# Seven-product stage of a decoder layer: deviation ahead of the first column tile, first pair's weights split there, products on banks apart

## The chip, the core and the metric

One Trainium2 chip, one core of it. The metric is the device time of one execution in microseconds (us); of several executions the median counts.

## The reference, cut to what matters

One layer of a decoder works on 520 tokens (512 of a prompt, 8 of decoding) with 1024 channels in fp32. The change touches the last of its sub-layers alone:

```python
h3 = rms_norm(x, lw['norm_ffn_g'])
x = x + jnp.square(jax.nn.relu(h3 @ lw['w_up'])) @ lw['w_down']      # 1024 -> 4096 -> 1024
```

Ahead of it come a mixing layer and a cross attention, which end with `x = x + om @ w_xo`.

## The kernel before, in words

All activations lie channel by channel: a tile is 128 channels (partitions) by 520 tokens, in two halves of 260. Each fp32 factor is cut into a high and a low part of type fp32r (`hilo` for tokens: ScalarE copies the high part, VectorE subtracts; `split_weights` for weights), and a product is made of three matmuls, high by high, high by low, low by high (`mm3`, L263). A weight tile is 128 x 1024. Its low part is made in one of two ways: `low` on VectorE (L178), or, for `wup` and `wdn`, a negated copy by ScalarE (L221) to which a DMA that GpSimd issues adds the weights from memory (L222). `weights` keeps LA = 3 entries of a written order split ahead.

The stage (from L1375 on) has 32 column tiles of `w_up`, in eight groups of four, and after each group four calls of `down`, each with one tile of `w_down` for two of the eight output tiles. A `down` has 48 matmuls.

- Group 0: four column tiles by plain products (`run("wup", i, ...)`, 48 matmuls each). They use tokens that aren't divided by their deviation yet; `post_up` does that afterwards: Relu (L1423), times `Rf` (L1427), Square (L1417), `hilo`. `Rf` is made by `rstd` in `post_up(0)`: four summing matmuls (L286) over the squares in `acc`, then ScalarE (L293 to L297) and VectorE (L298, L299).
- `forms` (L1391) makes the token side of the other groups, in four steps: per step two tiles times gain and `Rf` (L1396), four sums of halves (L1404 to L1407), and the cutting of all seven operands into high and low. FTB of its tiles lie in the pool `fp`, the others among the 37 tiles of `HL`.
- Groups 1 to 7: two calls of `up_pair` each. A pair is two column tiles by two token halves, made by a scheme of seven half-size products in place of eight (`product`, 12 matmuls each, in the order a, b, e, c, d, f, h), with VectorE's sums (`add`, L1450; L1475, L1476) between them. `split_pair` prepares its weights: two raw tiles `w` loaded by the queue SP issues (L184), four sums (L191), and the cutting into high and low (L197, L178).

PSUM has eight banks: two `g` tiles of two banks, three `m` tiles of one, one `d` tile of one. In a pair b and e are the two banks of one `g` tile, f and h those of another, a, c, d are `m` tiles. In a `down` one output tile is a `g` tile and the other is two `m` tiles; `post_down` adds them to the residual (L1492 for `g`, L1488 twice for `m`).

The order of each engine's instructions is fixed when the program is built, by a list scheduler that goes by program order, by `high_priority` (which moves a block ahead by AHEAD = 60 places) and by its own model of when an operand is ready. Each engine then works its list in order. Raw weight tiles share three buffers (`WB[0]`), the high and the low parts of single tiles three each, the sums' high and low parts three (`WB2`).

Of the kernel before, what the change touches and what calls it, by code (L numbers as in the profile page):

```python
# [9 lines left out]
F32 = mybir.dt.float32  # L10
# [7 lines left out]
P = 128  # L18
# [5 lines left out]
KT = 8  # L24
# [4 lines left out]
LA = 3  # L29
HLB = 37  # L30
WB2 = 3
FTB = 9
CR = "k0 k1 q0 q1 q2 q3 k2 v0 v1 k3 v2 v3"
ZS = [0, 0, 0, 1, 0, 1, 1, 1, 1, 1, 1, 1, 1, 1, 1, 1, 0, 1, 1, 1, 0, 1, 1, 0, 1, 0]
WARM = 2
# [62 lines left out]
def layer(ctx: ExitStack, tc: tile.TileContext, I: dict, O: dict):  # L98
# [13 lines left out]
    def gtile():  # L112
        return pg.tile([P, 2, 512], F32, tag="g", name="g")

    def mtile():
        return pm.tile([P, 512], F32, tag="m", name="m")
# [4 lines left out]
    def T(dt=F32, n=NT, bufs=TB):  # L121
        return tp.tile([P, n], dt, tag="t", name="t", bufs=bufs)
# [39 lines left out]
    CP = (0, 2, 1, 3)  # L162
    order += [("wup", i) for i in range(4)] + [("wdn", c) for c in CP]
    for g in range(1, 8):
        order += [("pair", 2 * g), ("pair", 2 * g + 1)] + [("wdn", 4 * g + c) for c in CP]
    order.reverse()
    ahead = []

# [10 lines left out]

    def split_pair(i):  # L180

        w = [wp.tile([P, KT, P], F32, tag="w", name="w", bufs=WB[0]) for _ in range(2)]
        for t, j in zip(w, (2 * i, 2 * i + 1)):
            SP.dma_start(out=t, in_=I["wup"][j].rearrange("p (k c) -> p k c", k=KT))  # L184
        lo4, hi4 = slice(0, 4), slice(4, 8)
        A11, A12, A21, A22 = w[0][:, lo4], w[0][:, hi4], w[1][:, lo4], w[1][:, hi4]
        pa, pb = [fp.tile([P, KT, P], F32, tag="p", name="p", bufs=2) for _ in range(2)]
        P1, P3, P2, P4 = pa[:, lo4], pa[:, hi4], pb[:, lo4], pb[:, hi4]

        def plus(out, a, b):  # L190
            free.add(V.tensor_tensor(out=out, in0=a, in1=b, op=ALU.add).ins.name)  # L191

        def split(src, pool, tag, bufs):
            shape = [P, src.shape[1], P]
            h = pool.tile(shape, F32R, tag="wh" + tag, name="wh", bufs=bufs)
            l = pool.tile(shape, F32R, tag="wl" + tag, name="wl", bufs=bufs)
            S.copy(h, src)  # L197
            low(l, src, h)
            return [(h[:, n:n + 4], l[:, n:n + 4]) for n in range(0, src.shape[1], 4)]

        a11, a12 = split(w[0], wp, "", WB[1])
        plus(P1, A21, A22)
        plus(P2, P1, A11)
        plus(P4, P2, A12)
        p2, p4 = split(pb, fp, "2", WB2)
        plus(P3, A11, A21)
        p1, p3 = split(pa, fp, "2", WB2)
        a22, = split(A22, fp, "3", 1)
        return a11, a12, a22, p1, p2, p3, p4

    def split_weights(name, i):
        if name == "pair":
            return split_pair(i)
        src = I[name][i]
        w = wp.tile([P, KT, P], F32, tag="w", name="w", bufs=WB[0])
        SP.dma_start(out=w, in_=src.rearrange("p (k c) -> p k c", k=KT))
        wh = wp.tile([P, KT, P], F32R, tag="wh", name="wh", bufs=WB[1])
        wl = wp.tile([P, KT, P], F32R, tag="wl", name="wl", bufs=WB[2])
        S.copy(wh, w)  # L219
        if name in ("wup", "wdn"):  # L220
            S.activation(wl, w, AF.Copy, scale=-1.0)  # L221
            GP.dma_start(out=wl, in_=src.rearrange("p (k c) -> p k c", k=KT), accum_op=ALU.add)  # L222
        else:
            low(wl, w, wh)
        return wh, wl
# [85 lines left out]
    def rstd(mat, srcs, n, y, v=None):  # L311

        v, a = v if v is not None else T(), T()
        rsqrt(colsum(mat, srcs), n, v, y, a[:, 0:NT])
        return v
# [1075 lines left out]
    def forms():  # L1391

        for k in range(4):
            n, m, t, u = T(), T(), T(), T()
            for o, i in ((n, k), (m, k + 4)):
                V.scalar_tensor_tensor(out=o, in0=x2[i], scalar=col("gffn", i), in1=Rf, op0=ALU.mult, op1=ALU.mult)  # L1396
            B11, B12, B21, B22 = n[:, A0[1]], n[:, A1[1]], m[:, A0[1]], m[:, A1[1]]
            if k % 2 == 0:
                b11 = form(2)
            sl = slice(k % 2 * H2, k % 2 * H2 + H2)  # L1400
            hilo(B11, b11[0][:, sl], b11[1][:, sl])
            X["B11", k] = b11[0][:, sl], b11[1][:, sl]
            N1, T2, T3, T4 = t[:, A0[1]], t[:, A1[1]], u[:, A0[1]], u[:, A1[1]]
            V.tensor_tensor(out=N1, in0=B11, in1=B12, op=ALU.subtract)  # L1404
            V.tensor_tensor(out=T2, in0=B22, in1=N1, op=ALU.add)
            V.tensor_tensor(out=T3, in0=B22, in1=B12, op=ALU.subtract)
            V.tensor_tensor(out=T4, in0=T2, in1=B21, op=ALU.subtract)  # L1407
            for src, names in ((t, ("N1", "T2")), (u, ("T3", "T4")), (m, ("B21", "B22"))):
                hi, lo = form(2)
                hilo(src, hi, lo)  # L1410
                for j, s in zip(names, (A0[1], A1[1])):
                    X[j, k] = hi[:, s], lo[:, s]
            yield
# [6 lines left out]
    def post_up(i):  # L1420
        def post(ps):
            r = T()
            S.activation(two(r), gv(ps), AF.Relu)  # L1423
            if i == 0:
                rstd(ones, [acc], D, T(), Rf)
                flows.append(forms())
            V.tensor_tensor(out=r, in0=r, in1=Rf, op=ALU.mult)  # L1427
            ups[0][i] = HL(), HL()
            rest(r, ups[0][i])
            yield  # L1430
        return post
# [4 lines left out]
            xh, xl = X[x, k]  # L1436
            PE_last[0] = mm3([(ps, (slice(None), slice(None)))], w[0][:, k], w[1][:, k], xh, xl, k == 0, k == 3)

    def up_pair(p):

        a11, a12, a22, p1, p2, p3, p4 = weights("pair", p)
        g, n = p // 2, p % 2 * 2
        a, c, d, be, fh = mtile(), mtile(), mtile(), gtile(), gtile()
        a, b, c, d, e, f, h = (x[:, 0:H2] for x in (a, be[:, 0], c, d, be[:, 1], fh[:, 0], fh[:, 1]))
        t, u, v = T(), T(), T()
        s1, u2, u3, c21, c22 = t[:, A0[1]], t[:, A1[1]], u[:, A0[1]], v[:, A0[1]], v[:, A1[1]]

        def add(out, x, y, op=ALU.add):
            with tc.high_priority(offset=AHEAD):
                V.tensor_tensor(out=out, in0=x, in1=y, op=op)  # L1450

        product(a, a11, "B11")
        if fresh[0]:
            advance()
        with tc.high_priority(offset=AHEAD):
            S.copy(s1, a)
        product(b, p2, "T2")
        add(u2, s1, b, ALU.subtract)
        product(e, p3, "T3")
        add(u3, e, u2)  # L1460
        product(c, p1, "N1")
        add(c22, c, u3)
        add(u2, c, u2)
        product(d, a22, "T4")
        add(c21, d, u3)
        with tc.high_priority(offset=AHEAD):
            S.activation(v, v, AF.Relu, scale=-1.0)
            ups[g][n + 1] = HL(), HL()
            rest(v, ups[g][n + 1])
        product(f, a12, "B21")  # L1470
        product(h, p4, "B22")

        def post():
            r = T()
            V.tensor_tensor(out=r[:, A0[1]], in0=f, in1=s1, op=ALU.add)  # L1475
            V.tensor_tensor(out=r[:, A1[1]], in0=h, in1=u2, op=ALU.add)  # L1476
            S.activation(r, r, AF.Relu)
            ups[g][n] = HL(), HL()
            rest(r, ups[g][n])
            yield  # L1480
        take(post())

# [15 lines left out]
    def down(g, cp):  # L1498

        W = weights("wdn", 4 * g + cp)  # L1500
        cs = (2 * cp, 2 * cp + 1)
        pss = [gtile(), [mtile(), mtile()]]

        def part(n, ks, first, last):
            for i, k in enumerate(ks):
                gemm(pss[n], (W[0][:, 4 * n:], W[1][:, 4 * n:]), ups[g][k:k + 1], first=first and i == 0,
                     last=last and i == len(ks) - 1, k0=k)

        if cp == CP[0] and g:
            for n in range(2):  # L1510
                part(n, (0, 1, 3), True, False)
            for n in range(2):
                part(n, (2,), False, True)
                take(post_down(g, cs[n])(pss[n]))
        elif g == 7 and cp == CP[-1]:
            part(0, range(4), True, True)
            take(post_down(g, cs[0])(pss[0]))
            gemm(pss[1], (W[0][:, 4:], W[1][:, 4:]), ups[g], apart=True)
            take(post_down(g, cs[1])(pss[1]))
        else:  # L1520
            for n in range(2):
                part(n, range(4), True, True)
                take(post_down(g, cs[n])(pss[n]))

    for i in range(4):
        run("wup", i, x2s, post_up(i))
    go()
    for g in range(8):
        for p in (2 * g, 2 * g + 1) if g else ():
            up_pair(p)  # L1530
        if g:
            flush()
        for c in CP:
            down(g, c)
# [99 lines left out]
```

## Time and profile before

| | us |
|---|---|
| median of 3 runs | 1054.37 |
| the three runs | 1052.58, 1054.37, 1057.49 |
| the profiled execution | 1050.55 |
| its span, first to last instruction | 1048.9 |

The profiled execution is the one that all rows below come from. PE is TensorE's matmuls, PEld its weight loads, DVE VectorE, ACT ScalarE, POOL GpSimd, SP the engine that issues plain loads. A row of the timeline begins with start and duration in us, and ends with the idle time of its engine ahead of it, and what ended that. A matmul's row lasts longer than the distance to the next one, since matmuls overlap.

### The profile page before, as it was taken

The page shows a single profiled execution, that of the slowest core. Times are in us where ns is not written, and L with a number is a line of the kernel's source. Part 1 is how long each engine was busy: PE and PEld are TensorE (multiplying, and loading weights), DVE is VectorE, ACT ScalarE, POOL GpSimd, SP SyncE. Part 2 cuts the span into 40 slices and gives each one's busy share as a digit, 9 for nine tenths or more (in the row PEclk, how much of TensorE's full clock was granted, in tenths as well). Part 3 has the DMA queues.
Part 4 walks back from the last instruction along what each step waited for, and adds up shares of the span by engine and source line. Part 5 has one row for each costly group of instructions (what it writes and reads, how often), then busy time and mean ns, then how long its engine had stood idle before and what let it go on. Part 6 is the DMA issues. An engine that isn't in the chain of part 4 may idle for free.

```text
span 1048.9 us, 21539 instructions
## 1 busy us (share of the span) xinstructions
PE 1027.3 (98%) x8266; PEld 944.3 (90%) x8266; DVE 660.8 (63%) x1220; ACT 537.1 (51%) x876; POOL 173.2 (17%) x303
## 2 busy tenths in 40 slices
PE   9999999999999999999999999998999999999998
PEld 8977877789988889889999986997999999999998
DVE  7757677677555666434776687679465565656553
ACT  7755567854221235314455686684646446464452
POOL 1333443231223323320000000010000000000000
PEclk9999999999999999999999999999999999999999
DMA  8877986575557767762622575385556565665644
GB/s 295 313 247 246 260 284 218 170 201 168 181 192 243 246 204 222 236 197 81 212 85 98 193 247 184 86 168 130 143 148 139 155 140 121 153 147 147 157 102 122
DMA packets 62665, 190.97 MB, mean 182 GB/s; under 512 B 10209, under 2 KB 13026, under 8 KB 62434
## 3 DMA queue, kind: packets, MB, share of 16 engines
q0 software_dynamic: 25984, 87.07, 32.0%
q1 hardware_dynamic: 36578, 102.52, 28.9%
q8 instruction: 65, 1.06, 0.4%
q14 instruction: 38, 0.31, 0.1%
HBM read 183.94 MB, written 5.61 MB: 181 GB/s over the span
## 4 chain that ended last, share of the span: by engine, by line
PE 71%; DVE 10%; DMA 9%; ACT 6%; issue 2%; SPq 0%; DVEq 0%; ACTq 0%
PE g L263 50%; PE m L263 10%; DMA w<-in_wup 7%; PE d L600 3%; DVE p L191 3%; PE d L548 2%; PE m L286 1%; DMA w<-in_win 1%; ACT wh L219 1%; DVE wl L178 1%; PE g L1171 1%; DVE hl L146 1%; ACT wl L221 1%; DMA wl<-in_wdn 1%; DVE hl L1492 1%
## 5 line engine op out<-in xcount | busy, mean ns | idle before, releaser
L263 PE MATMUL g<-hl,wh 128*128 128x260 f32 x3664 | 609.9, 285 | 5.0 <-DVE hl L146 1.8
L263 PEld LDWEIGHTS g<-hl,wh 128*128 128x128 f32 x3664 | 511.4, 189 | 23.3 <-issue 7.0
L263 PE MATMUL g<-hl,wl 128*128 128x260 f32 x1832 | 385.2, 283 | 1.4 <-DMA wl<-in_wdn 1.4
L263 PEld LDWEIGHTS g<-hl,wl 128*128 128x128 f32 x1832 | 289.1, 189 | 1.8 <-DMA wl<-in_wdn 1.6
L219 ACT CAST wh<-w 128x1024 fp32r<-128x1024 f32 x126 | 131.8, 1047 | 244.0 <-PE g L263 116.3
L178 DVE TENSOR_TENSOR wl<-w,wh 128x1024 fp32r<-128x1024 f32 (+1 forms) x118 | 136.4, 1157 | 33.3 <-ACT wh L219 31.0
L263 PE MATMUL m<-hl,wh 128*128 128x260 f32 x736 | 127.8, 283 | 3.6 <-DVE hl L1488 3.6
L263 PEld LDWEIGHTS m<-hl,wh 128*128 128x128 f32 x736 | 105.7, 188 | 4.8 <-DVE hl L1488 4.8
L513 POOL DMA_DIRECT2D pg<-in_vc x128 | 68.8, 538 | 176.3 <-issue 78.6
L513 POOL DMA_DIRECT2D pg<-in_kc x128 | 68.9, 539 | 144.8 <-issue 99.3
L263 PE MATMUL m<-hl,wl 128*128 128x260 f32 x368 | 84.5, 283 | 1.2 <-DMA wl<-in_wdn 1.2
L222 POOL DMA_DIRECT2D wl<-in_wdn x32 | 27.6, 864 | 311.5 <-ACT wl L221 188.6
L475 DVE TENSOR_TENSOR t<-g,R 128x520 f32<-128x520 f32 x48 | 33.4, 695 | 64.1 <-PE g L263 64.1
L197 ACT CAST wh<-p 128x1024 fp32r<-128x1024 f32 x28 | 28.8, 1048 | 84.2 <-DVE p L191 58.2
L146 DVE TENSOR_TENSOR hl<-t,hl 128x520 fp32r<-128x520 f32 (+3 forms) x65 | 42.6, 657 | 33.5 <-ACT hl L145 33.2
L263 PEld LDWEIGHTS m<-hl,wl 128*128 128x128 f32 x368 | 61.0, 188 | 1.4 <-DMA wl<-in_wdn 1.4
L145 ACT CAST hl<-t 128x520 fp32r<-128x520 f32 (+3 forms) x65 | 37.8, 588 | 13.5 <-DVE t L486 11.3
L882 DVE SCALAR_TENSOR_TENSOR hl<-uc,cols,hl 128x512 f32<-128x512 f32 x60 | 41.2, 745 | 0.0
L221 ACT ACTIVATE wl<-w 128x1024 fp32r<-128x1024 f32 x36 | 37.9, 1053 | 0.0
L178 DVE TENSOR_TENSOR wl<-p,wh 128x1024 fp32r<-128x1024 f32 x28 | 33.7, 1223 | 5.6 <-ACT wh L197 5.6
L191 DVE TENSOR_TENSOR p<-w 128x512 f32<-128x512 f32 x28 | 19.3, 690 | 25.6 <-DMA w<-in_wup 25.6
L222 POOL DMA_DIRECT2D wl<-in_wup x4 | 3.5, 866 | 188.1 <-DVE ss L1199 176.2
(297 smaller groups left out, 1221.7 us busy)
## 6 DMA issues: line engine op xcount, KB each, us to landing
pg<-in_kc POOLq DMA_DIRECT2D x128, 256.0 KB, 4.4
pg<-in_vc POOLq DMA_DIRECT2D x128, 256.0 KB, 4.0
w<-in_win SPq DMA_DIRECT2D x56, 512.0 KB, 4.6
w<-in_wup SPq DMA_DIRECT2D x32, 512.0 KB, 3.9
w<-in_wdn SPq DMA_DIRECT2D x32, 512.0 KB, 3.9
wl<-in_wdn POOLq DMA_DIRECT2D x32, 512.0 KB, 7.9
w<-in_wo SPq DMA_DIRECT2D x8, 512.0 KB, 3.3
hl<-in_cmk SPq DMA_DIRECT2D x16, 256.0 KB, 5.8
```

Of the source, the lines that this page charges most:

```text
L145: S.copy(hi, src)
L146: V.tensor_tensor(out=lo, in0=src, in1=f(hi), op=ALU.subtract)
L178: free.add(V.tensor_tensor(out=wl, in0=w, in1=f(wh), op=ALU.subtract).ins.name)
L191: free.add(V.tensor_tensor(out=out, in0=a, in1=b, op=ALU.add).ins.name)
L219: S.copy(wh, w)
L221: S.activation(wl, w, AF.Copy, scale=-1.0)
L222: GP.dma_start(out=wl, in_=src.rearrange("p (k c) -> p k c", k=KT), accum_op=ALU.add)
L263: m = PE.matmul(o, lhsT=w, rhs=x[sl], start=first and n == 0, stop=last and n == 2)
L475: V.tensor_tensor(out=two(t), in0=gv(ps), in1=two(Rt), op=ALU.mult)
L513: last.append(GP.dma_start(out=dst, in_=src[bass.ds(pid, 1)].rearrange("o p f -> p o f")))
L600: PE.matmul(ps[32 * i:32 * i + 32, :], lhsT=Dt[:, n, :], rhs=vp[:, i, :], start=n == 0, stop=n == 15)
L882: V.scalar_tensor_tensor(out=y[:, 0:NP], in0=u[:, k:k + NP], scalar=cw[:, k:k + 1], in1=y[:, 0:NP], op0=ALU.mult, op1=ALU.add)
```

## The change

- `rstd` moves out of `post_up(0)` to ahead of the first column tile, under `high_priority`.
- `split_pair(2)`, the weights of the first pair, is called there too. Its raw tiles lie in the pool `fp`, in two buffers of their own (so do those of every even pair; odd pairs stay with the three shared ones), and the parts of its first raw tile lie with those of the sums. FTB falls from 9 to 5 to make room.
- Column tiles 0 and 1 run interleaved (`pair`): for each of the eight input tiles first the matmuls of one, then of the other. `forms` is stepped at written places: after them, after tile 2, and twice after tile 3.
- `wup` in group 0 gets its low part on VectorE, not by ScalarE and a DMA.
- In a pair, a goes to the `d` tile, b, c, e to `m` tiles, d to a `g` tile of its own; f and h share one as before.
- For the second pair of a group Relu and Square of one of the results become one VectorE instruction. In group 0 the first `down` takes the last column tile last, for both output tiles.

```diff
-FTB = 9
+FTB = 5
-        order += [("pair", 2 * g), ("pair", 2 * g + 1)] + [("wdn", 4 * g + c) for c in CP]
+        order += [("pair", p) for p in (2 * g, 2 * g + 1) if p > 2] + [("wdn", 4 * g + c) for c in CP]
     def split_pair(i):
-        w = [wp.tile([P, KT, P], F32, tag="w", name="w", bufs=WB[0]) for _ in range(2)]
+        w = [(wp if i % 2 else fp).tile([P, KT, P], F32, tag="w", name="w", bufs=WB[0] if i % 2 else 2) for _ in range(2)]
-        a11, a12 = split(w[0], wp, "", WB[1])
+        a11, a12 = split(w[0], wp, "", WB[1]) if i > 2 else split(w[0], fp, "2", WB2)
     def split_weights(name, i):
-        if name in ("wup", "wdn"):
+        if name == "wdn":
     def post_up(i):
-            if i == 0:
-                rstd(ones, [acc], D, T(), Rf)
-                flows.append(forms())
-    def up_pair(p):
-        a11, a12, a22, p1, p2, p3, p4 = weights("pair", p)
+    def up_pair(p, W):
+        a11, a12, a22, p1, p2, p3, p4 = W
-        a, c, d, be, fh = mtile(), mtile(), mtile(), gtile(), gtile()
-        a, b, c, d, e, f, h = (x[:, 0:H2] for x in (a, be[:, 0], c, d, be[:, 1], fh[:, 0], fh[:, 1]))
+        a, b, c, e, d, fh = dtile(), mtile(), mtile(), mtile(), gtile(), gtile()
+        a, b, c, d, e, f, h = (x[:, 0:H2] for x in (a, b, c, d[:, 0], e, fh[:, 0], fh[:, 1]))
...
-            S.activation(r, r, AF.Relu)
             ups[g][n] = HL(), HL()
-            rest(r, ups[g][n])
+            if n:
+                V.scalar_tensor_tensor(out=r, in0=r, scalar=0.0, in1=r, op0=ALU.max, op1=ALU.mult)
+                hilo(r, *ups[g][n])
+            else:
+                S.activation(r, r, AF.Relu)
+                rest(r, ups[g][n])
     def down(g, cp):
-        if cp == CP[0] and g:
+        if cp == CP[0]:
+            late = 2 if g else 3
             for n in range(2):
-                part(n, (0, 1, 3), True, False)
+                part(n, [k for k in range(4) if k != late], True, False)
             for n in range(2):
-                part(n, (2,), False, True)
+                part(n, (late,), False, True)
-    for i in range(4):
-        run("wup", i, x2s, post_up(i))
+    with tc.high_priority(offset=AHEAD):
+        rstd(ones, [acc], D, T(), Rf)
+    first_pair = split_pair(2)
+    made = forms()
+    pair([("wup", 0), ("wup", 1)], x2s, [post_up(0), post_up(1)])
+    next(made)
+    run("wup", 2, x2s, post_up(2))
+    next(made)
+    run("wup", 3, x2s, post_up(3))
     go()
+    next(made)
+    next(made)
+    next(made, None)
     for g in range(8):
         for p in (2 * g, 2 * g + 1) if g else ():
-            up_pair(p)
+            up_pair(p, first_pair if p == 2 else weights("pair", p))
```

## Rows read from the trace of the kernel before

**Rows 1.** The page: span, busy time by engine, and the raw weight loads of `w_up`.
```profile
span 1048.9 us, 21539 instructions
PE 1027.3 (98%) x8266; PEld 944.3 (90%) x8266; DVE 660.8 (63%) x1220; ACT 537.1 (51%) x876; POOL 173.2 (17%) x303
...
w<-in_wup SPq DMA_DIRECT2D x32, 512.0 KB, 3.9
```

**Rows 2.** Three windows: length, busy time and count by engine, clock, DMA share, GB/s.
```profile
664.05:681.30 17.25, 17.25 (x143) 17.25 (x144) 12.34 (x18) 12.93 (x19) 1.76 (x2) 1.00 0.50 127
...
708.59:729.55 20.96, 15.84 (x123) 14.94 (x123) 20.68 (x38) 12.32 (x18) 1.69 (x2) 1.00 0.58 127
776.55:999.03 222.48, 219.52 (x1800) 216.97 (x1800) 132.62 (x231) 113.40 (x151) 17.28 (x20) 1.00 0.59 143
```

**Rows 3.** Chain of waits, a piece near its end: start, duration, engine, line, count.
```profile
1037.05 2.87 PE m L263 x24
```

**Rows 4.** Waits of PE from 700 us on: total, times, longest.
```profile
PE m L263 <- DVE hl L1488: 3.6, 6, 0.8
PE g L263 <- DVE hl L146: 1.8, 1, 1.8
PE g L263 <- DMA wl<-in_wdn: 1.4, 1, 1.4
PE m L263 <- DMA wl<-in_wdn: 1.2, 1, 1.2
PE g L263 <- ACT hl L145: 0.7, 1, 0.7
```

**Rows 5.** Timeline, third product of pair 2, and the start of pair 4.
```profile
738.10 0.42 DVE L1450 TENSOR_TENSOR t<-t,g 128x260 f32<-128x260 f32 x1
...
738.58 0.51 PE L263 MATMUL g<-x,wh 128*128 128x260 f32 x2
...
779.42 0.40 PE L263 MATMUL m<-x,wh 128*128 128x260 f32 x2
...
780.16 0.76 DVE L1488 TENSOR_TENSOR x<-m,x 128x260 f32<-128x260 f32 x2
```

**Rows 6.** Timeline at the end of group 1, DVE and PE.
```profile
773.06 0.69 DVE L191 TENSOR_TENSOR p<-w 128x512 f32<-128x512 f32 x1 [3.35 <-DMA w<-in_wup]
...
776.08 0.76 DVE L1488 TENSOR_TENSOR hl<-m,hl 128x260 f32<-128x260 f32 x2
...
776.55 0.63 PE L263 MATMUL m<-hl,wh 128*128 128x260 f32 x3 [0.62 <-DVE hl L1488]
```

**Rows 7.** Timeline of group 0, several engines.
```profile
692.40 0.70 DVE L298 TENSOR_TENSOR t<-t,R 128x520 f32<-128x520 f32 x1 [6.94 <-ACT t L297]
...
708.45 0.59 ACT L1423 ACTIVATE t<-g 128x520 f32<-128x520 f32 x1
...
718.37 0.52 PE L263 MATMUL g<-hl,wh 128*128 128x260 f32 x2 [1.77 <-DVE hl L146]
...
722.30 0.86 POOL L222 DMA_DIRECT2D wl<-in_wdn  x1 [12.88 <-ACT wl L221]
...
729.55 0.51 PE L263 MATMUL g<-hl,wl 128*128 128x260 f32 x2 [1.41 <-DMA wl<-in_wdn]
```

**Rows 8.** Groups by shape, 681.3 to 735 us: count, busy us, mean ns, idle before.
```profile
L146 DVE TENSOR_TENSOR hl<-t,hl 128x520 fp32r<-128x520 f32 x13 | 9.2, 705 | 0.0
...
L219 ACT CAST wh<-w 128x1024 fp32r<-128x1024 f32 x7 | 7.3, 1046 | 8.7 <-PE m L263 6.4 <-PE g L263 1.4 <-ACT t L1198 0.7
...
L1396 DVE SCALAR_TENSOR_TENSOR t<-hl,cols,R 128x520 f32<-128x520 f32 x4 | 3.0, 761 | 0.0
...
L191 DVE TENSOR_TENSOR p<-w 128x512 f32<-128x512 f32 x4 | 2.8, 695 | 0.9 <-DMA w<-in_wup 0.9
...
L178 DVE TENSOR_TENSOR wl<-w,wh 128x1024 fp32r<-128x1024 f32 x2 | 2.4, 1216 | 0.0
...
L1404 DVE TENSOR_TENSOR t<-t 128x260 f32<-128x260 f32 x4 | 1.7, 429 | 0.0
```

## The prediction, on record before the changed kernel ran

> **What bounds the kernel.** Read the page first: TensorE's matmuls are busy for 1027.3 of 1048.9 us [rows 1], so time can only come from the matmuls' count, their pace, or gaps between them. The change keeps every matmul. The windows then give the granted clock, 1.00 in each [rows 2], the 2.4 GHz level, so nothing is to be had there. Pace: 143 matmuls in 17.25 us without a gap are 0.1206 us each [rows 2], 24 in 2.87 are 0.1196 [rows 3]; I take 0.120. With it the windows show where matmuls are not back to back. Five groups, 1800 matmuls (per group 2 x 84 + 4 x 48 = 360 by the code), want 216.0 us and took 222.5: **1.3 us lost per group**. From 708.59 to 729.55, in group 0, 123 matmuls want 14.8 us and took 21.0: **6.2 us lost** [rows 2].
>
> The list of waits says on what [rows 4]. Six times PE waits for L1488, the reading of two `m` tiles: 3.6 us idle, 0.6 each. Idle time understates a wait: two matmuls last 0.40, so a row of one is 0.28 long and runs 0.16 past the next one's due start, and the first two after a wait last 0.51, 0.11 more [rows 5]. So each costs about 0.86, together 5.2. The rest of the 1.3, 0.44 per group, is the third product of the pairs. Group 0 waits for tokens cut late (L145, L146: 2.5 us idle) and for DMAs that finish `wl` (2.6 us idle) [rows 4].
>
> Ceiling of the gain: 6 x 0.86 = 5.2, 7 x 0.44 = 3.1 (I use 2.9, as the pace may be 0.1206), and 6.2: **14.3 us**.
>
> **The change, part by part.** *Raw weights of even pairs in their own buffers.* In the timeline VectorE, which works its list in order, sits 3.35 us in L191 until the second raw tile of the odd pair has landed; the L1488 that PE needs stands behind four such sums and starts at 776.08, PE at 776.55 [rows 6]. A load lands 3.9 us after issue [rows 1], so it was issued late: with three shared buffers the odd pair's tiles wait until the even pair's are split. With two more buffers the odd pair's tiles wait only for `wdn` tiles that are split some 20 us before the group's end, by order of the buffers. The load then lands well ahead and L191 no longer holds L1488. Gain between 0 (another item of the list takes L191's place) and 5.2; I take 4.7, as in no other of a group's `down` calls does PE wait for an evacuation.
> The Trainium skill has the rule beneath this: "ScalarE/VectorE/GpSimdE queues are strict FIFO" (PSUM — Partial Sum Buffer, section Engine vs sequencer instructions). The rows above agree with it. The same rule speaks against the change, for everything newly put into VectorE's list holds what is behind it; that is the first and the last rival below.
>
> *Each product on a bank apart.* The third product begins at 738.58, just after VectorE has read the second one's bank (738.10 + 0.42) [rows 5]: b and e are two banks of one tile, and the program orders them by tile. Apart, e waits for no reading: 2.9 us over seven groups. From the other side: e now wants one of three `m` tiles, two of which the last `down` has just filled (last rival); for b and c the same tiles come free a product or more ahead, and a's `d` tile is used by nobody else. Floor 0, ceiling 2.9; I take 2.9.
> By the Trainium skill (PSUM — Partial Sum Buffer, section PSUM bank collisions raise a hardware error) only accesses to the same bank have to be kept apart, so the chip did not ask for this wait. By that alone the part is worth 0, and by the row 2.9; the wait in the row decides.
>
> *Group 0, VectorE's list.* It idles 6.94 us for the deviation's chain on ScalarE [rows 7] and is then full: 20.68 of 20.96 us in the window in which PE starves [rows 2]. Work from 685 us to pair 3's second product, by the groups' means [rows 8]: `forms`, per step 2 x 0.76 + 5 x 0.43 + 3 x 0.70 = 5.8, four steps 23.0; four `post_up` of 2 x 0.70, 5.6; two pairs' weights of 4 x 0.69 + 3.5 x 1.22 = 7.1, 14.2; the deviation 1.4; eight outputs added, 5.9. New: low parts of `wup` 2 and 3, 2.4 (those of 0 and 1 go to the stage before, where VectorE idles 4.9 of 17.25 us [rows 2]). Sum 52.5. Time until that product: four tiles and four `down` are 384 x 0.120 = 46 us from 681.3, the pair's 7 products 10, one more 1.4, so 739: 54 us. It fits, barely, because the first pair's 7.1 us now fill the 6.94 us of idling, and because the column tiles' chains run ahead of the forms by priority. Tile 3's chain then is Relu 0.59 [rows 7], two passes of VectorE and two of ScalarE of 0.6 to 0.7 [rows 8], some 3.6 us; in the trace it took from 708.45 to 718.37, 10 us [rows 7]. The first `down` has 36 matmuls, 4.3 us, ahead of the first that reads tile 3. So the tokens' wait goes or leaves up to 1.5 us.
> DMA waits: both came from a late split (wl issued at 722.30, read at 729.55, 7.25 later [rows 7]). Four such transfers of `wup` leave GpSimd's queue, nothing is put ahead. But tiles 0 and 1 now end together, so the buffers for tile 3's and the first `wdn`'s parts come free together: the `wdn` follows one cast of 1.05 [rows 8] and two Relus of 0.59 later than alone, 2.2 us; its wl is due 11.5 us after, of which 7.25 + 2.1 are used. Between 0 and 1.5.
> New wait: at the same point both `g` tiles are full, so tile 2's first matmul waits for the first Relu. That tile ends 6 matmuls, 0.72 us, earlier; 0.3 to notice, 0.59 to run [rows 7], 0.1 restart: 0.3 us, or 1.3 behind a cast. Behind it stand all later column tiles.
> SP: two loads of 3.9 us [rows 1] move from group 0 to ahead of the `wdn` loads; DMA share is 0.50 there [rows 2], no price. The tokens' 24 `HL` tiles, 8 of group 0 and 4 residuals make 36 of 37: steps 3 and 4 wait for tile 3's operands to go, which the 54 us contain.
> Left over in group 0: 0.3 to 4.3 us; I take 1.5, nearest to the sum of the low ends plus one priority slip.
>
> *One VectorE instruction for Relu and Square* in odd pairs: 7 x 0.76 more on VectorE [rows 8], which has 132.6 of 222.5 us busy there [rows 2]; two ScalarE passes less on a chain that PE doesn't wait for. Nothing.
>
> **Sum.** 14.3 - 1.5 (group 0) - 0.5 (boundary) = 12.3 us. On the profiled execution, 1050.55 us (1.65 around its span): 1038.2. The median, 1054.37, lies 3.8 above that execution; the same difference from it gives **1042**.
>
> **Rivals.**
> 1. *VectorE stays the bound of group 0*: 52.5 us in 54 leave no room, tile 3 or the forms come late, the 6.2 are lost as before. For it: the 20.68 of 20.96. Against: 6.94 idle us are filled. 12.3 - 4.7 = 7.6: 1046.8. Chance 0.14.
> 2. *The boundary's wait stays*: another item holds L1488 (a low part, 1.22, waiting for ScalarE). 12.3 - 4.7 = 7.6: 1046.8. Chance 0.09.
> 3. *It doesn't do what it says*: the scheduler's list puts the first pair's weights and the sums where they were; only the 2.9 of the banks come. 1051.5. Chance 0.07.
> 4. *Slower*: the third product of each even pair waits for `m` tiles. It starts 2.88 us after the last `down` ends (the next one's first matmul stands at 779.42); L1488 ended at 780.92, 1.5 after [rows 5]. Every low part of 1.22 that the list puts ahead of L1488 adds as much: from the second on PE waits, at three it is 1.5 + 3.66 - 2.88 + 0.1 = 2.4, times seven 16.7: 1042 + 16.7 = 1058.7; at four 1067. A pair's weights are 3.5 such parts. Against: with the raw tiles early these parts are done before the boundary. I name 1059. Chance 0.06.
>
> **Numbers.** Forecast 1042, chance 0.64, own range 1038 (ceiling 14.3, and the fastest run 1.8 under the median) to 1046 (group 0 at 4.3, boundary half). Rivals 1 and 2 reach to 1049 with two us of the runs' spread; 1038 to 1049.5 leaves out rivals 3 and 4 and little else. A measurement of this kernel can tell about 0.5%, 5.3 us: faster is below 1049.1. Forecast 0.64, most of rivals 1 and 2, 0.18: 0.82. Same 0.12, slower 0.06.
>
> **What would show it.** Right: no wait of PE for L1488 at the groups' ends, no L191 that idles for `w`; five groups in 216 to 218 us; e starting with no idle time; group 0 from the last column tile to pair 2 in about 24.5 us. A short wait of PE for L1423 after the first two column tiles shows the price of running them together. Wrong: waits of `m` matmuls in the third product, waits for `wl<-in_wdn` at the first `down`, a wait for the forms at pair 2, or longer pace with the same count of matmuls.

## The result, and the profile after

The changed kernel takes 1042.8 us in the median of four executions (1040.07, 1042.72, 1042.87, 1044.78) against 1054.19 for the kernel before beside it: a ratio of 0.9886, 95% interval 0.9853 to 0.9919. Timed again later, six executions have a median of 1040.64, ratio 0.9884, interval 0.9858 to 0.9911. The forecast was 1042, faster.

The page of after, part 1, answering [rows 1]; the profiled execution is the one of 1040.07 us:

```profile
span 1038.4 us, 21502 instructions
...
PE 1020.9 (98%) x8266; PEld 941.1 (91%) x8266; DVE 669.4 (64%) x1231; ACT 525.8 (51%) x858; POOL 170.3 (16%) x299
```

The same 8266 matmuls. To see where the time came from, cut the stage in two: its first 388 matmuls, as many as four column tiles, the deviation (four) and four `down` have (called **group 0** from here on), and the other 2520 (**groups 1 to 7**). The cut goes by count: in some of the kernels up to twelve matmuls of the first pair stand ahead of it, and as many of a `down` behind it. At 0.120 us each these want 46.6 and 302.4. Windows between the starts of those matmuls, columns as in [rows 2]; before:

```profile
681.42:734.93 53.51, 48.39 (x390) 47.16 (x389) 43.97 (x78) 35.02 (x52) 5.16 (x6) 1.00 0.67 147
734.93:1045.39 310.46, 306.88 (x2521) 303.51 (x2520) 176.51 (x310) 154.19 (x205) 24.20 (x28) 1.00 0.58 141
```

and after:

```profile
682.71:732.50 49.79, 47.40 (x391) 46.87 (x390) 42.87 (x76) 33.71 (x51) 4.33 (x5) 1.00 0.57 140
732.50:1034.91 302.41, 302.41 (x2521) 302.41 (x2520) 180.99 (x317) 144.19 (x188) 23.36 (x27) 1.00 0.58 140
```

Groups 1 to 7 gave 8.05 us and now run at the matmuls' pace without a gap. Group 0 gave 3.72, and 3.2 are still lost in it. The stage is 11.8 us shorter; the span only 10.5, because the stage begins 1.29 us later (682.71 against 681.42). After is 1.28 us behind already at the program's 350th matmul, and in other executions of kernels with this change the stage began at 681.0 to 683.7, so that part is scatter of what comes ahead.

The waits of PE in after from 680 us on, answering [rows 4] (in total, times, longest), are two:

```profile
PE g L263 <- DMA wl<-in_wdn: 1.7, 1, 1.7
PE g L263 <- ACT t L1423: 0.7, 1, 0.7
```

**The boundary of a group.** (Lines have moved by one to three: L1488 is L1489 now, L1492 is L1493, L1427 is L1424.) The timeline of after, where a later group stands as group 1 does in [rows 6]; rows of DVE, SP and PE:

```profile
852.53 1.22 DVE L178 TENSOR_TENSOR wl<-w,wh 128x1024 fp32r<-128x1024 f32 x1
...
853.77 0.33 SPq L184 DMA_DIRECT2D w<-in_wup  x1
...
857.19 0.69 DVE L191 TENSOR_TENSOR p<-w 128x512 f32<-128x512 f32 x1 [2.82 <-DMA w<-in_wup]
857.80 0.76 DVE L1489 TENSOR_TENSOR hl<-m,hl 128x260 f32<-128x260 f32 x2
...
859.23 0.64 PE L263 MATMUL m<-hl,wh 128*128 128x260 f32 x4
```

VectorE still idles at L191 for a raw tile, nearly as long as the 3.35 us of before. But the L1489 that PE needs stands right behind the first sum, not behind four sums and a reading of a `g` tile, and is done 0.67 us ahead of the matmul that takes the `m` tiles.

**Group 0.** The timeline of after, several engines, answering [rows 7]:

```profile
691.29 0.70 DVE L298 TENSOR_TENSOR t<-t,R 128x520 f32<-128x520 f32 x1 [1.06 <-ACT t L297]
...
694.30 1.05 ACT L219 CAST wh<-w 128x1024 fp32r<-128x1024 f32 x1 [3.04 <-PE g L263]
695.25 0.60 ACT L1423 ACTIVATE t<-g 128x520 f32<-128x520 f32 x1
...
695.90 0.74 PE L263 MATMUL g<-hl,wh 128*128 128x260 f32 x4 [0.67 <-ACT t L1423]
...
702.57 1.05 ACT L219 CAST wh<-w 128x1024 fp32r<-128x1024 f32 x1
...
705.72 0.86 POOL L222 DMA_DIRECT2D wl<-in_wdn  x1 [6.75 <-ACT wl L221]
...
712.73 0.51 PE L263 MATMUL g<-hl,wl 128*128 128x260 f32 x2 [1.72 <-DMA wl<-in_wdn]
```

VectorE's 6.94 us of idling ahead of L298 are 1.06, with 2.65 more ahead of the low part of column tile 3 (at 695.38). The deviation's four matmuls run at the same place in both kernels, 4.9 us into the stage. Earlier is what follows on ScalarE: with no weight's cast and no Relu between its steps any more, L297 ends 8.6 us into the stage and not 11.0. PE's wait for tokens is gone. Two waits are new or left: for the first Relu after the two interleaved tiles, which stands behind a cast, and for the low half of the second `w_down` tile.

### The profile page after: what moved, and what is told of

Read it like the earlier page. It is cut to its first block, busy times and chain, and to the rows that moved or that the text cites. A ratio compares the mean times of both kernels' runs of the same rounds, so it can differ in the third digit from the quotient of the medians.

```text
span 1038.4 us, 21502 instructions
## 1 busy us (share of the span) xinstructions
PE 1020.9 (98%) x8266; PEld 941.1 (91%) x8266; DVE 669.4 (64%) x1231; ACT 525.8 (51%) x858; POOL 170.3 (16%) x299
## 3 DMA queue, kind: packets, MB, share of 16 engines
q8 instruction: 65, 1.06, 0.4%
## 4 chain that ended last, share of the span: by engine, by line
PE 89%; ACT 4%; DVE 4%; DMA 1%; issue 1%; SPq 0%; DVEq 0%; ACTq 0%
PE g L263 60%; PE m L263 15%; PE d L600 3%; PE d L548 2%; PE d L263 2%; PE m L286 2%; PE g L1171 1%; ACT wh L219 1%; DVE wl L178 1%; DMA wl<-in_wdn 1%; DMA hl<-in_xT 1%; PE m L653 1%; PE m L701 0%; PE m L687 0%; PE m L708 0%
## 5 line engine op out<-in xcount | busy, mean ns | idle before, releaser
L178 DVE TENSOR_TENSOR wl<-w,wh 128x1024 fp32r<-128x1024 f32 (+1 forms) x122 | 141.3, 1160 | 37.1 <-ACT wh L219 33.9
L263 PE MATMUL m<-hl,wh 128*128 128x260 f32 x792 | 134.8, 282 | 0.0
L263 PEld LDWEIGHTS m<-hl,wh 128*128 128x128 f32 x792 | 114.0, 188 | 0.0
L263 PE MATMUL m<-hl,wl 128*128 128x260 f32 x396 | 92.4, 282 | 0.0
L263 PEld LDWEIGHTS m<-hl,wl 128*128 128x128 f32 x396 | 66.2, 188 | 0.0
L146 DVE TENSOR_TENSOR hl<-t,hl 128x520 fp32r<-128x520 f32 (+3 forms) x67 | 43.6, 654 | 20.6 <-ACT hl L145 20.2
L197 ACT CAST wh<-w 128x1024 fp32r<-128x1024 f32 (+1 forms) x28 | 23.3, 835 | 39.8 <-PE m L263 30.1
L191 DVE TENSOR_TENSOR p<-w 128x512 f32<-128x512 f32 x28 | 19.0, 688 | 26.6 <-DMA w<-in_wup 26.6
L221 ACT ACTIVATE wl<-w 128x1024 fp32r<-128x1024 f32 x32 | 33.7, 1054 | 0.0
```

The source lines that it names most:

```text
L146: V.tensor_tensor(out=lo, in0=src, in1=f(hi), op=ALU.subtract)
L178: free.add(V.tensor_tensor(out=wl, in0=w, in1=f(wh), op=ALU.subtract).ins.name)
L263: m = PE.matmul(o, lhsT=w, rhs=x[sl], start=first and n == 0, stop=last and n == 2)
```

## Experiments: the two parts that rule groups 1 to 7

My theory gave the banks 2.9 us and the raw buffers 4.7 to 5.2, each for itself. The first four kernels undo or do one part alone. All tables and windows below use the cut above.

**The old banks in the kernel after**

```diff
-        a, b, c, e, d, fh = dtile(), mtile(), mtile(), mtile(), gtile(), gtile()
+        a, c, d, be, fh = mtile(), mtile(), mtile(), gtile(), gtile()
```

> The changed kernel with the PSUM tiles of a pair as before: b and e two banks of one tile, a, c, d on m tiles. Theory (the third product's wait comes from two banks in one tile): about 0.25 us before the third product of the first pair of a group and 0.16 of the second return, 0.4 per group, 2.9 in seven groups, and the waits at the groups' ends stay away; span about 1041.3 against 1038.4. Rival (the waits at the groups' ends depend on which product takes the m tiles): those return too, 0.86 each, six of them, span about 1046.5.

Measured: 1044.79 us. Its two windows:

```profile
682.45:734.57 52.12, 47.70 (x391) 46.96 (x389) 42.84 (x76) 33.41 (x50) 4.33 (x5) 1.00 0.54 140
734.57:1039.63 305.06, 305.06 (x2521) 303.06 (x2520) 181.32 (x317) 144.22 (x189) 23.37 (x27) 1.00 0.57 137
```

and among PE's waits one of group 0 that after does not have:

```profile
PE g L263 <- DVE hl L1493: 1.1, 1, 1.1
```

Groups 1 to 7 take 2.65 us more (302.41 to 305.06), with no wait of theirs in the list: at the third product of each pair the first two matmuls start 0.16 to 0.27 and 0.23 after the one ahead of them, in place of 0.12, which isn't counted as idle time. In group 0 a wait for the reading of a `g` tile (L1493) appears, 1.1 us.

**Even pairs' raw tiles back in the three shared buffers**

```diff
-        w = [(wp if i % 2 else fp).tile(..., bufs=WB[0] if i % 2 else 2) for _ in range(2)]
+        w = [(wp if i != 2 else fp).tile(..., bufs=WB[0] if i != 2 else 2) for _ in range(2)]
```

> The changed kernel with the raw tiles of all pairs but the first back in the three shared buffers. Theory (late raw tiles of the odd pair hold VectorE's list at the group's end): six waits of PE for L1489 return, 0.86 each, 5.2 in all, span about 1043.6, and VectorE idles about 3 us in L191 within 5 us of each group's end. Rival (the waits went because the list of VectorE came out in another order, for another reason): no wait returns, span 1038 to 1039. The changed kernel's VectorE idles as long in L191 as before, 26.6 us, which speaks for the rival.

Measured: 1046.31 us. The window of groups 1 to 7:

```profile
733.82:1041.15 307.33, 304.00 (x2521) 302.54 (x2520) 180.82 (x317) 143.47 (x188) 23.32 (x27) 1.00 0.58 141
```

PE's longest entry in the list of waits:

```profile
PE m L263 <- DVE hl L1489: 3.2, 5, 1.0
```

and VectorE's timeline at the same boundary as above:

```profile
859.78 0.69 DVE L191 TENSOR_TENSOR p<-w 128x512 f32<-128x512 f32 x1 [3.20 <-DMA w<-in_wup]
860.39 0.69 DVE L1493 TENSOR_TENSOR hl<-g,hl 128x520 f32<-128x520 f32 x1
861.00 0.68 DVE L191 TENSOR_TENSOR p<-p,w 128x512 f32<-128x512 f32 x1
861.60 0.68 DVE L191 TENSOR_TENSOR p<-w 128x512 f32<-128x512 f32 x1
862.20 0.69 DVE L191 TENSOR_TENSOR p<-p,w 128x512 f32<-128x512 f32 x1
862.80 0.76 DVE L1489 TENSOR_TENSOR hl<-m,hl 128x260 f32<-128x260 f32 x2
```

Groups 1 to 7 take 4.92 us more, the boundary's wait is back, and with it the four sums ahead of L1489. VectorE's idle time at L191 is about that of after (28.2 us in all from 735 us on, against 26.6); what the buffers change is what stands behind the load in VectorE's list.

The load itself changes too. From the DMA issues of a stretch (KB each, us from issue to landing), the load that such a sum waits for, in before:

```profile
w<-in_wup SPq DMA_DIRECT2D x1, 512.0 KB, 7.9
```

in the kernel with shared buffers, and then in after:

```profile
w<-in_wup SPq DMA_DIRECT2D x1, 512.0 KB, 7.8
```

```profile
w<-in_wup SPq DMA_DIRECT2D x1, 512.0 KB, 3.3
```

A window from the load's issue to its landing, columns as above, in before, with shared buffers, and in after:

```profile
765.04:772.96 7.92, 7.92 (x69) 7.92 (x68) 4.67 (x6) 2.47 (x3) 0.00 (x0) 1.00 0.86 239
```

```profile
851.90:859.70 7.80, 7.76 (x65) 7.56 (x64) 4.68 (x6) 2.38 (x3) 0.00 (x0) 1.00 0.89 219
```

```profile
853.77:857.10 3.33, 3.33 (x30) 3.33 (x30) 0.60 (x1) 0.76 (x1) 0.00 (x0) 1.00 0.57 172
```

With shared buffers that load is issued within two us of another raw load and of the DMA that finishes a `wl`, and needs 7.8 to 7.9 us with the DMA engines 0.86 to 0.89 busy; so it does at all six boundaries of before (7.4 to 7.9). In after the loads that a sum waits for took 3.3 to 5.2. The Trainium skill says that transfers issued from several engines run on the same DMA engines and interleave (DMA: Bandwidth & Descriptors, section Issuing engines are not separate DMA queues); these three loads agree.

But the shorter load is no gain by itself, for it is issued that much later. The first `m` matmul of the `down` in question, in before and with shared buffers (in after it is the one at 859.23, above):

```profile
775.66 0.28 PE L263 MATMUL m<-hl,wh 128*128 128x260 f32 x1
```

```profile
862.04 0.28 PE L263 MATMUL m<-hl,wh 128*128 128x260 f32 x1
```

The sum that waits begins 2.60 us ahead of it in before (at 773.06), 2.26 with shared buffers, and 2.04 in after. At all the boundaries at which it waits these are 2.4 to 2.8, 2.3 to 3.1 and 2.0 to 2.7. So the raw tile comes no earlier than it did, for the matmul that hangs on it, and the gain is in the list's order alone, which is fixed when the program is built: from that sum's end to the reading it holds 2.4 us of other work in before (773.66 to 776.08) and none in after. By these rows, as an estimate, the old order would have L1489 begin at some 860.2 in after, and PE wait. Why the scheduler lays the list out so once two buffers are added, no run shows.

**The new banks in the kernel before**

```diff
-        a, c, d, be, fh = mtile(), mtile(), mtile(), gtile(), gtile()
+        a, b, c, e, d, fh = dtile(), mtile(), mtile(), mtile(), gtile(), gtile()
```

> The kernel before with the PSUM tiles of the changed one, nothing else. Theory: 0.4 per group gone, 2.9 in all, span 1046 against 1048.9, six waits for L1488 stay. Rival (banks alone carry the steady groups' gain): 8.1 gone, span 1040.8.

Measured: 1048.09 us, windows:

```profile
681.17:736.72 55.55, 49.92 (x390) 48.68 (x389) 43.96 (x78) 35.00 (x53) 5.16 (x6) 0.97 0.65 143
736.72:1042.93 306.21, 304.29 (x2522) 303.05 (x2520) 175.72 (x310) 154.15 (x205) 24.18 (x28) 1.00 0.58 143
```

Groups 1 to 7 gain 4.25, more than the 2.65 that undoing the banks costs after: the boundary's waits shrank as well (PE idle for L1488 1.9 us, five times, against 3.6 [rows 4]). Alone, the banks don't help group 0: without the spell of half clock in it (below, 1.6) it takes about 54, before 53.5.

**Both undone, so that only the changes for group 0 stand**

```diff
-        w = [(wp if i % 2 else fp)...
+        w = [(wp if i != 2 else fp)...
...
-        a, b, c, e, d, fh = ...
+        a, c, d, be, fh = ...
```

> The changed kernel with both the PSUM tiles and the shared raw buffers as before, so that of the change only group 0's part is left. Theory: the parts add up, 8.1 us of the gain are lost, span about 1046.5, and group 0 loses 2.9 us as in the changed kernel. Rival (group 0's order also cures the groups' ends): span 1041 to 1042, only the third products' waits return.

Measured: 1051.28 us; the window of groups 1 to 7:

```profile
736.09:1046.10 310.01, 306.74 (x2521) 303.15 (x2520) 181.45 (x317) 143.83 (x189) 23.30 (x27) 1.00 0.57 138
```

Groups 1 to 7 lose 7.60, and 2.65 + 4.92 = 7.57: undone in the new kernel the two parts add up, and nothing else in the change matters there. Group 0 takes 53.74, or 52.1 without a spell of half clock in it, as with the old banks alone (52.12).

## Experiments: group 0

**The deviation back behind the first Relu**

```diff
             S.activation(two(r), gv(ps), AF.Relu)
+            if i == 0:
+                rstd(ones, [acc], D, T(), Rf)
...
-    with tc.high_priority(offset=AHEAD):
-        rstd(ones, [acc], D, T(), Rf)
```

> The kernel after with the deviation's chain put back behind the Relu of column tile 0 (two lines moved), all else as it is. In the kernel after VectorE waits 1.06 us for this chain at 691.29; in the kernel before it waited 6.94 us at 692.40, with every sum of group 0 behind it. Theory that this wait was what the change shortened in group 0: VectorE stands about 6 us longer in front of the first tiles' sums, and since it is otherwise busy there, the downs of group 0 start late by 2 to 5 us; the stage from the first up matmul to the last is 354 to 357 us, and the program 2 to 5 us longer than after. Rival (VectorE has slack, and the banks alone made group 0 shorter): the stage stays within 0.5 us of after's 352.2.

Measured: 1046.46 us. The window of group 0:

```profile
683.69:738.87 55.18, 50.28 (x390) 48.72 (x389) 42.93 (x76) 33.33 (x51) 4.33 (x5) 0.97 0.50 129
```

and the timeline: VectorE ahead of the first tiles' sums, and the matmul that then waits for tokens:

```profile
696.41 1.23 DVE L178 TENSOR_TENSOR wl<-w,wh 128x1024 fp32r<-128x1024 f32 x1 [5.21 <-ACT wh L219]
700.48 0.70 DVE L298 TENSOR_TENSOR t<-t,R 128x520 f32<-128x520 f32 x1 [2.85 <-ACT t L297]
...
704.68 0.85 PE L263 MATMUL d<-x,wh 128*128 128x260 f32 x2 [1.74 <-ACT x L145]
```

Group 0 takes 55.2, or 53.6 without the spell in it (1.6): 2.7 to 3.8 more than in two executions of after. VectorE stands 8.1 us in front of the first tiles' sums, and PE waits for tokens again. So, with the tiles interleaved, group 0's gain needs the early deviation. That 53.6 comes near before's 53.5 is chance, for this is not the old place: with tiles 0 and 1 interleaved the first Relu comes later, and L298 begins 16.8 us into the stage here, 11.0 in before and 8.6 in after. How much of the gain against before the 2.4 us between the last two are worth isn't shown. The scheduler also lays out the list anew, so the two moved lines aren't the only difference.

**The first pair's weights split in turn, not ahead**

```diff
-        order += [("pair", p) for p in (2 * g, 2 * g + 1) if p > 2] + ...
+        order += [("pair", p) for p in (2 * g, 2 * g + 1)] + ...
-    first_pair = split_pair(2)
-            up_pair(p, first_pair if p == 2 else weights("pair", p))
+            up_pair(p, weights("pair", p))
```

> The changed kernel with the first pair's weights split in the written order again, after the third w_down tile, not ahead of the first column tile. Theory (VectorE's list is full from the deviation to the first pair, and 7.1 us of it were moved into its idle time): VectorE idles about 7 us more ahead of the deviation's product, and PE waits 1 to 5 us more at the end of group 0 or in the first pair, stage 353 to 357. Rival (there is room anyway): 352.2, no new wait.

Measured: 1043.31 us; group 0 has 53.41, groups 1 to 7 have 302.20. At face value this is the theory's time. But the edit didn't move the split. The low parts of the first pair's sums on VectorE, in after and then here:

```profile
684.85 1.22 DVE L178 TENSOR_TENSOR wl<-p,wh 128x1024 fp32r<-128x1024 f32 x1
...
687.27 1.22 DVE L178 TENSOR_TENSOR wl<-p,wh 128x1024 fp32r<-128x1024 f32 x1
```

```profile
687.09 2.35 DVE L178 TENSOR_TENSOR wl<-p,wh 128x1024 fp32r<-128x1024 f32 x2
```

In before they stood at 723.36 and 726.56, 42 us into the stage. Here the scheduler has put the whole split, from the loads on, ahead again by itself: PE's and ScalarE's lists are those of after from end to end, and VectorE's differs in four swaps. So this is the kernel after once more, and neither the theory nor the rival was tested by it.

What it adds is a third execution of after's lists. Its PE waits 2.59 us for `wl`, until 713.43, and a window that begins within that wait has the lower level of TensorE's clock:

```profile
712.81:719.64 6.83, 6.21 (x28) 6.21 (x29) 4.87 (x10) 1.75 (x4) 0.04 (x1) 0.50 0.69 152
```

Its 28 matmuls took 6.21 us where 0.120 each makes 3.4: 2.9 us. Without them group 0 has 50.5, and two executions of after have 49.8 and 50.9.

What the early split is worth therefore stays open. Rows speak for some of it. In before the sums of the first pair stand at 714.58, 715.79 and 717.00 in VectorE's list, 0.6 us each, ahead of the low part of tokens for which PE waits until 718.37 [rows 7]:

```profile
717.00 0.70 DVE L191 TENSOR_TENSOR p<-p,w 128x512 f32<-128x512 f32 x1
717.60 0.71 DVE L146 TENSOR_TENSOR hl<-t,hl 128x520 fp32r<-128x520 f32 x1
```

In after no part of a pair's split stands in that list between 689.1 and 726 us.

**The kernel after once more, and column tiles 0 and 1 one after the other.** Tiles in turn:

```diff
-    pair([("wup", 0), ("wup", 1)], x2s, [post_up(0), post_up(1)])
+    for i in range(2):
+        run("wup", i, x2s, post_up(i))
```

First, in one execution:

> The changed kernel with column tiles 0 and 1 one after the other in place of interleaved. Theory (both g tiles end together, so tile 2 waits for the first Relu behind a cast): the wait of PE for L1423, 0.67 idle, 0.93 with the restart, is gone, and the wait for the second w_down tile's low part, 1.72 idle, stays: the stage is 0.9 us shorter (352.2 from its first matmul to its last in the changed kernel, 351.3 here). Rival (the interleaving covers the last tokens of the stage before): a wait of 0.5 to 2 us stands at the stage's start instead, no gain or a loss.

Measured: 1039.17 us; group 0 48.50, groups 1 to 7 302.44; the wait for L1423 is gone, the one for `wl` 0.9. Then timed, in six executions each, beside the kernel after:

> The kernel after itself, unchanged, timed again beside the next two. Four runs so far: 1040.07 to 1044.78. Both theories of the next two expect 1040 to 1045 here.

Measured: median 1040.64. PE's waits in the stage differ from those of after's first trace in one row, the wait for the second `w_down` tile. PE's wait here:

```profile
PE g L263 <- DMA wl<-in_wdn: 2.8, 1, 2.8
```

and the DMA's time from issue to landing, here and in the first trace:

```profile
wl<-in_wdn POOLq DMA_DIRECT2D x1, 512.0 KB, 8.1
```

```profile
wl<-in_wdn POOLq DMA_DIRECT2D x1, 512.0 KB, 7.0
```

The same transfer, issued at the same point of the stage, took 7.0 and 8.1 us, and the wait follows it: 1.7 and 2.8.

> The kernel after with column tiles 0 and 1 computed one after the other, as the kernel before had them, and the rest as after. One look gave 1039.17 and a stage of 350.95 us against after's 352.21; the wait for tile 1's tokens (0.93 us) was gone and that for the second w_down tile's low half shorter. Theory that the pairing of the two tiles costs and gives nothing back: median 1.0 to 2.5 us under the kernel after beside it. Rival (the gap between single looks is the spread of runs): within 0.7 us of it.

Measured: median 1038.91, ratio to before 0.9864, interval 0.9840 to 0.9887. The median is 1.73 under the kernel after beside it; the means differ by 2.4, with a 95% interval of some 2.5 to each side, so the times alone just fail to tell it from nothing. The traces do: group 0 takes 48.50 and 48.47 us in two executions with tiles in turn, 49.79 and 50.89 in two of after and 50.5 in the third above, its spell left out. The timed kernel's window of group 0 and PE's wait that is left:

```profile
681.02:729.49 48.47, 47.64 (x391) 46.99 (x390) 43.31 (x76) 33.26 (x51) 4.33 (x5) 1.00 0.59 150
```

```profile
PE g L263 <- DMA wl<-in_wdn: 0.8, 2, 0.7
```

The wait for the Relu goes, and the one for the second `w_down` tile shrinks: its DMA leaves GpSimd 23.0 us into the stage in after (705.72 - 682.71), and 21.0 and 21.1 us into it with tiles in turn. No version run here was measurably shorter than this one.

**The second `w_down` tile's low half on VectorE**

```diff
-        if name == "wdn":
+        if name == "wdn" and i != 2:
```

alone, together with the tiles in turn, and that once more, timed:

> The changed kernel with the low part of the second w_down tile of group 0 made by VectorE (one instruction of 1.22 us) in place of ScalarE and a DMA. Theory (that DMA's 7 us after a late cast is what PE waits for at 712.73): the wait of 1.72 idle, 1.98 with the restart, is gone, stage 350.2 against 352.2. Rival (VectorE's list is what bounds group 0): 1.2 us more in it make the last column tile late by as much, PE waits for L146 instead, gain under 0.8.

> Both: tiles 0 and 1 one after the other, and the second w_down tile's low part on VectorE. Theory: the two gains add, stage 349.3 against 352.2, span about 1035.5 against 1038.4. Rival (VectorE's list bounds group 0): 351 or more, with waits for L146 or L145.

> As the kernel before this one, and the low half of the second w_down tile subtracted on VectorE instead of on GpSimd with its DMA. One look gave 1039.49, in which one steady group lost 0.92 us at a late load of wup. Theory that the two waits of group 0 are separate and both worth their length: 0.3 to 0.8 us under the tiles-in-turn kernel beside it. Rival (VectorE, the busier engine of group 0, passes the work on as a wait of its own): within 0.3 us of it or above.

Measured: alone 1039.29 us, group 0 48.85. The wait for `wl` is gone, but a wait of 0.4 for L1493 stands in its place, and the gain is half of what I expected. With the tiles in turn 1039.49 in one execution, 1039.02 in the median of six, against 1038.91 without it: no gain, as the rival expects, and a wait for L146 (0.4 us) in place of the DMA's, so VectorE passes the work on. In the one execution groups 1 to 7 took 303.58, for one late load. The same sum in the kernel with the tiles in turn alone, then here, with the matmul that waited:

```profile
844.93 0.69 DVE L191 TENSOR_TENSOR p<-w 128x512 f32<-128x512 f32 x1 [3.24 <-DMA w<-in_wup]
```

```profile
845.46 0.69 DVE L191 TENSOR_TENSOR p<-w 128x512 f32<-128x512 f32 x1 [4.63 <-DMA w<-in_wup]
...
847.15 0.63 PE L263 MATMUL m<-hl,wh 128*128 128x260 f32 x3 [0.92 <-DVE hl L1489]
```

VectorE idled 1.39 us longer and PE lost 0.92 of it: the margin there, in a group's second `down`, is about half a microsecond. At a group's end it can be thinner: in the second trace of after the sum that waits begins at one boundary only 1.02 us ahead of the first `m` matmul (815.51, 816.53), and PE just doesn't wait. The boundary's wait is not abolished; it has been moved just out of reach.

## Why the prediction was right, point by point

- **Ceiling and place.** The count, pace and clock left only gaps to gain: right. Of the 14.3 us, 11.8 came in the stage, against a forecast of 12.3.
- **Banks, 2.9.** Measured 2.65 by undoing them: the wait in the row was there to be gained. Not foreseen: in group 0 they take away another 1.1 (L1493), and done alone they also shorten the boundary's wait.
- **Raw buffers, 4.7 of 5.2.** Size right (4.92 by undoing), mechanism wrong. The failing step is "it was issued late ... The load then lands well ahead and L191 no longer holds L1488", and of the prediction's own signs "no L191 that idles for `w`" didn't come. The load of before was not issued late: it went out at 765.04, 10.6 us ahead of the `m` matmul, and took 7.9 us among others, where I had put the page's median of 3.9. After, it is issued 5.5 us ahead and takes 3.3, so it lands no earlier (L191 idles 26.6 us in all from 735 us on, before 24.7). The gain came another way, by the list: three fewer sums and one reading fewer stand between the load and L1489. That the size fitted is luck to this extent: it was the whole wait, whichever way it went. Which buffer the load is issued for at 853.77, 0.02 us after a low part of VectorE ended, the trace doesn't say, so "wait only for `wdn` tiles split some 20 us before" isn't borne out, and stays open.
- **Group 0, 4.7 of 6.2.** Measured 3.7 in the profiled execution, 2.6 in the second. VectorE's list fitted, as worked out, and tile 3's tokens came in time. "Because the first pair's 7.1 us now fill the 6.94 us of idling" is seen in part: 3.1 us of that pair's low parts stand there in after (684.85 to 689.09), the rest of its split earlier still. But the idling also ends sooner, as the deviation's chain ends 2.4 us earlier in the stage, which the prediction had not counted. With that chain late the gain is gone; what the split would cost late, no run shows.
- **Left over, 1.5.** This is the term that was mis-sized: 2.5 of the 6.2 us are left in the profiled execution, 3.6 in the second. The Relu behind a cast cost 0.83 (0.95 from one matmul's start to the next, less 0.12) (0.3 to 1.3 foreseen). The DMA's wait, taken as 0 to 1.5 for the first `w_down` tile, fell on the second: its cast stands on ScalarE between the forms' casts, its DMA leaves at 705.72 and takes 7.0 to 8.1, and PE loses 1.9 to 3.0. I had costed one tile of four.
- **The number.** 1042 against 1042.8 owes a little to offsetting: in the profiled execution groups 1 to 7 gave 8.05 for a forecast of 7.6, group 0 gave 3.7 for 4.7. The profiled execution itself, forecast at 1038.2, took 1040.07, with 1.29 of it from ahead of the stage.
- **Rivals.** VectorE as the bound of group 0: no, it idles 2.65 us there, and no matmul waits for cut tokens. The boundary's wait stays: no, though by half a microsecond or less. It doesn't do what it says: no. The third product waits for `m` tiles: no such wait in the list. On the chain for an added VectorE pass per odd pair: groups 1 to 7 run at pace, so nothing, as said.

## What to carry to other kernels

When an engine idles for a load and a reading that the matmuls need is queued behind it, count what stands between the two in its list: here the idle time stayed as it was, and 2.4 us of other work taken out from between them was worth 4.9 us over six boundaries. A load can take twice the median of its kind (7.9 us, where the page gives 3.9), so look up its own row and what was in flight beside it; and hold its landing against the start of the matmul that hangs on it before putting a gain down to the load. Before reading an experiment's time, see in its trace whether the edit did anything: one here was meant to move work back and left it where it was. Of several like transfers at a start cost each, for the last on its engine's list is the one that comes late.

## What the hardware showed that I had not expected

Some executions have short stretches in which the granted clock is 0.50, the 1.2 GHz level. Where PE is busy, a short one costs about 1.6 us (15 to 17 matmuls start 0.215 to 0.218 apart, not 0.120), the longer one above 2.9. The four of them in group 0 begin within a wait of PE of 1.7 to 2.8 us (the long one, in that of 2.59) or up to 1.1 us behind its end. But waits as long brought none in after (1.72 and 2.8), with the old banks (2.7) and with shared buffers (2.8), and in others one came near 641 or 268 us, in parts that all these kernels share. The times of one kernel follow the mean clock: the six executions of after timed together run from 1038.27 at 1.000 over 1040.6 at 0.998 to 1044.87 at 0.996. As an estimate, 0.004 of 1040 us is 4.2 of the 6.6 us between them.
